# A two-block transformer step in split fp32: rounded-weight products with 512 moving columns in place of 256

## Chip, cores and metric

One NeuronCore of a Trainium2 chip. The metric is the device time of one execution in microseconds, here of the only core. `kernel` packs the weights on the host, builds one program and launches it once.

## What is computed

One batch row of 256 tokens and 1024 features goes through block 1 twice (its two layers) and then through block 2 twice. All inputs and the output are fp32. Cut to what matters:

```python
def layer_1(x):                       # twice
    s1, k1, g1, s2, k2, g2 = split(silu(c) @ w_ada + b_ada, 6)
    z = modulate(rmsnorm(x), s1, k1) @ w_in          # 1024 -> 2284 columns
    x = x + g1 * (concat(swa(z), mla(z), nsa(z), moba(z)) @ w_out)
    u = relu(modulate(rmsnorm(x), s2, k2) @ w_up) ** 2     # 1024 -> 4096
    return x + g2 * (u @ w_down)                           # 4096 -> 1024

def layer_2(x, mem):                  # twice
    z, xs, bc, dt, dq, dk, dv, dg, cq, cg, gl = split(x @ w_in_2)
    mk, mv = split(mem @ w_mem_kv)
    y = rmsnorm(ssd_scan(conv(xs), conv(bc), dt) * silu(z))     # 32 heads
    d = diff_attention(rope(dq), rope(dk), dv) * silu(dg)       # 8 heads
    q = cross_attention(cq, mk, mv) * silu(cg)                  # 4 heads
    g = sigmoid(gl + gate_b)                                    # three gates
    o = g[0] * (y @ w_br_ssd) + g[1] * (d @ w_br_diff) + g[2] * (q @ w_br_cross)
    return layernorm(alpha * x + o @ w_out_2)
```

## The kernel before, in words

Activations lie feature-major: a tile of 128 features by 256 tokens, eight of them for the 1024 features. A product with a weight keeps nearly fp32 accuracy by splitting both sides into a rounded part (type fp32r, one pass of the array) and the rest: `ah`, `al` for activations, `wh`, `wl` for weights, and summing `wh*ah + wh*al + wl*ah` in PSUM.

The weights come through one stream. `stream` (L269) lists weight groups of 1024x256 in the order of their use; each is two tiles `w` of 128x1024 (512 KB), loaded by SP's queue up to `AHEAD_W` = 8 tiles ahead (`_fetch`, L273). Up to four tiles ahead `_split` (L282) rounds them: ScalarE writes `wh` (L290), VectorE the rest `wl` (L292), both put ahead of other work by `high_priority`.

`gemm` (L320) is the product. It takes one of three `g` banks of PSUM (128x512 fp32) and walks two pieces, one per weight tile; each has four slices `k` of 128 input features and two halves `c` of the output, and each of these issues three matmuls of 256 columns through `mm` (L317): `wh` with `ah`, `wh` with `al`, `wl` with `ah`. With `tok=True` the sides are swapped: the activation slice is the weight of the array and 256 weight columns move, so that tokens lie on partitions. After the last piece `evac` reads the whole bank: a copy (`cq` L1244, `mk` L439, the block-1 projections L687 and L688), a `relu` and its square (L966 to L971), a `silu` (`silu2`, L1108), a gate's `tanh` (L1374), or a multiplication into the sum of branches (L1381 to L1388).

The pieces are put into a queue (`add`, L305) and the program calls `fill(n)` and `need(tag)` between the steps of attention, scan and norms, so that TensorE has products to run while the other engines work. From this emission order a scheduler sets the final order on each engine; engines run their lists in order.

The down product of the MLP (`down`, L975), the causal convolutions' products (`xs`, `bc`), `dt`, and `w_out1` have their own PSUM layout or readers and also use 256 columns. In block 2 the 32 scan heads (`scan_a`, `scan_b`) alternate with the pieces of `cg`, `gl`, `br2`, `xs`, `dq` and `dk`, the eight heads of the differential attention (`diff`, L1538) with those of `z` and `br0`; the products of `dg`, `gl`, `br1` and `out` follow one another.

Of the kernel before, what the change touches and what calls it, by code (L numbers as in the profile page):

```python
# [58 lines left out]
def _pack_in(w):  # L59

    L, K, M = w.shape
    r = w.reshape(L, K // P, P, M // 256, 256).transpose(0, 3, 2, 1, 4)
    return np.ascontiguousarray(r).reshape(L, M // 256, P, -1)

# [69 lines left out]
def _pack(inp):  # L134
# [39 lines left out]
    for key, n0, n in (("z", 0, 2048), ("xs", 2048, 2048), ("bc", 4096, 1024), ("dq", 5184, 1024), ("dk", 6208, 1024),  # L174
                       ("dv", 7232, 1024), ("dg", 8256, 1024), ("cq", 9280, 1024), ("cg", 10304, 1024), ("gl", 11328, 3072)):
        o["w2_" + key] = _pack_in(cut(n0, n))
    dt = np.concatenate([cut(5120, 64), np.zeros((DEPTH, D, 64), np.float32)], 2)
    o["w2_dt"] = dt.reshape(DEPTH, KC, P, P).transpose(0, 2, 1, 3).reshape(DEPTH, P, 1024)
    o["w2_mem"] = _pack_in(a["w_mem_kv_2"])
# [4 lines left out]
    o["w2_out"] = _pack_in(a["w_out_2"])  # L184
# [21 lines left out]
NW, NS = 8, 4  # L206
AHEAD_W, AHEAD_S = 8, 4
# [5 lines left out]
flat = lambda tl: tl.rearrange("p a b -> p (a b)")  # L213


class Emit:
# [52 lines left out]
    def stream(self, *keys):  # L269
        for key in keys:  # L270
            self.wq.extend([key, i, None, None] for i in range(1 if key[0] == "w2_dt" else 2))
# [48 lines left out]
    def gemm(self, tag, keys, act, evac, tok=False, half=None):  # L320
# [6 lines left out]
        def piece(n):  # L327
# [4 lines left out]
            ah, al = act(n // 2)  # L332
            for k in range(4):
                kk = (n % 2 if half is None else half) * 4 + k
                for c in range(2):
# [3 lines left out]
                    if tok:  # L339
                        sl = slice(k * 256, (k + 1) * 256)  # L340
                        ts = slice(c * P, (c + 1) * P)
                        self.mm(o, ah[:, kk, ts], wh[:, sl], st, False)
                        self.mm(o, al[:, kk, ts], wh[:, sl], False, False)
                        self.mm(o, ah[:, kk, ts], wl[:, sl], False, sp)
                    else:
                        sl = slice(k * 256 + c * P, k * 256 + (c + 1) * P)
                        self.mm(o, wh[:, sl], ah[:, kk, :], st, False)
                        self.mm(o, wh[:, sl], al[:, kk, :], False, False)
                        self.mm(o, wl[:, sl], ah[:, kk, :], False, sp)
# [3 lines left out]
        for n in range(last + 1):  # L353
            self.add(tag, lambda n=n: piece(n))
# [72 lines left out]
def load_mem(e):  # L427
    mf = v3(e.unit("mf"), KC)
    mh, ml = v3(e.unit("mh", F32R), KC), v3(e.unit("ml", F32R), KC)
    for k in range(0, KC, 4):  # L430
        e.nc.sync.dma_start(mf[:, k : k + 4, :], e.d["memT"][:, k : k + 4, :])
        e.split(mh[:, k : k + 4, :], ml[:, k : k + 4, :], mf[:, k : k + 4, :])
    return mh, ml


def mem_gemm(e, l, g, hl, mk, mv, tag="mem"):

    if g < 4:
        ev = lambda ps: e.nc.scalar.copy(mk[:, 2 * g : 2 * g + 2, :], v3(ps, 2))  # L439
    else:  # L440
        ev = lambda ps: e.nc.scalar.copy(mv[:, :, (g - 4) * 256 : (g - 3) * 256], v3(ps, 2))
    e.gemm(tag, [("w2_mem", l, g)], lambda i: hl, ev, tok=g >= 4)
# [3 lines left out]
def block1(e, ctx, mem0):  # L446
# [3 lines left out]
    mhl, mk0, mv0 = mem0  # L450
# [14 lines left out]
    MEM = 6  # L465
    a0 = ada(0, 0) + ada(0, 1)
    start = [[], a0[0:2], a0[2:4], a0[4:6], a0[6:8], []]
    for k in range(MEM):
        e.stream(("w2_mem", 0, k), *start[k])
# [13 lines left out]
    e.stream(*[("w2_mem", 0, k) for k in range(MEM, 8)])  # L483
# [63 lines left out]
    def norm_apply(src, bc, A, sh, ah, al):  # L547
        with tc.high_priority(offset=NORM_FIRST):
            for k in range(KC):
                tt = e.t(ap_, [P, S], "nt", bufs=2)  # L550
                nc.vector.scalar_tensor_tensor(tt, src[:, k, :], A[:, k : k + 1], bc[:, :S], ALU.mult, ALU.mult)
                nc.scalar.activation(ah[:, k, :], tt, AF.Identity, bias=sh[:, k : k + 1])  # L552
                nc.vector.scalar_tensor_tensor(al[:, k, :], tt, sh[:, k : k + 1], ah[:, k, :].bitcast(F32), ALU.add, ALU.subtract)  # L553


    for g in range(MEM):
        mem_gemm(e, 0, g, mhl, mk0, mv0, f"start{g}")
# [27 lines left out]
    class Attend:  # L585
# [70 lines left out]
        def out(self, put=None):  # L656
# [7 lines left out]
            if self.last:  # L664
                oh, ol, base = put
                for c in range(2):
                    e.split(oh[:, base + c, :], ol[:, base + c, :], o[c][:, :S])

    def mixers(l, ah, al, oh, ol, ev_x):
# [9 lines left out]
        def ev_c(ps):  # L679
# [6 lines left out]
        act = lambda i: (ah, al)  # L686
        dv = lambda dst: (lambda ps: nc.vector.tensor_copy(dst, ps if len(dst.shape) == 2 else v3(ps, 2)))  # L687
        sc = lambda dst: (lambda ps: nc.scalar.copy(dst, v3(ps, 2)))  # L688
        evs = {0: ("A", dv(zA)), 1: ("B", dv(zB)), 2: ("C", ev_c), 3: ("H", dv(vn)), 5: ("E", sc(qa)), 4: ("D", sc(qn)),
               6: ("F", sc(qm)), 7: ("G", dv(km)), 8: ("I", sc(vm))}  # L690
# [984 lines left out]
```

## Time and profile before

| | |
|---|---|
| time, median of 3 runs | 1840.06 us (1837.85 to 1841.8) |
| the profiled execution | 1838.83 us |
| its span, first to last instruction | 1837.0 us |
| TensorE busy | 98% of the span, 14800 records |
| VectorE / ScalarE / POOL busy | 73% / 55% / 20% |
| mean granted TensorE clock | 0.992 |
| read from HBM | 339 MB |

PE is TensorE's matmul, PEld its weight load (beside it), DVE is VectorE, ACT ScalarE, SP the engine that issues the loads. A name such as `g<-ah,wh` says which tiles an instruction writes and reads, without buffer numbers; a matmul's duration in the trace is a modelled latency, so the price of one in a stream is the distance between starts. Plain fp32 matmuls (attention scores, transposes) are recorded as two instructions.

### The profile page before, as it was taken

The numbers are of one execution on the slowest core, as the hardware profiler recorded it, in microseconds if no ns is written. First come the engines' busy times: TensorE is split into PE (matmuls) and PEld (weight loads), VectorE is DVE, ScalarE is ACT, GpSimd is POOL, SyncE is SP. The second block draws the span as 40 slices with busy tenths as digits, with TensorE's granted clock in tenths as the row PEclk, the third lists the DMA queues.
The fourth block names the chain that finished last, engine by engine and source line by source line (L and its number), as shares of the span: only waits on it lengthen the run. The fifth ranks groups of instructions, "written<-read, shape, count | busy, mean of one in ns | idle before, by whom it ended". The sixth has DMA issues, their size and how long they took to land.

```text
span 1837.0 us, 37186 instructions
## 1 busy us (share of the span) xinstructions
PE 1791.6 (98%) x14800; PEld 1696.7 (92%) x14800; DVE 1334.8 (73%) x2212; ACT 1017.1 (55%) x1882; POOL 358.9 (20%) x291
## 2 busy tenths in 40 slices
PE   7999999999998999999999999999999999999998
PEld 6878799987878999999999999999999999999998
DVE  4575775756778655798897897566687897997566
ACT  4354444444545444557777575454556687675552
POOL 0000271800007300002444202200001445202200
PEclk9999999999998999999999999999999999999999
DMA  9873886757447655554444644465553445554451
GB/s 335 317 246 129 301 272 197 258 197 294 130 138 282 230 182 183 168 171 140 143 162 154 191 161 148 166 205 175 193 175 130 148 160 162 181 166 168 153 183 60
DMA packets 98223, 346.88 MB, mean 189 GB/s; under 512 B 12288, under 2 KB 13440, under 8 KB 97792
## 3 DMA queue, kind: packets, MB, share of 16 engines
q1 hardware_dynamic: 98048, 344.50, 55.5%
q8 instruction: 116, 1.90, 0.4%
q14 instruction: 59, 0.48, 0.1%
HBM read 339.01 MB, written 1.05 MB: 185 GB/s over the span
## 4 chain that ended last, share of the span: by engine, by line
PE 90%; DVE 3%; ACT 2%; DMA 2%; issue 1%; POOL 0%; POOLq 0%; SPq 0%; DVEq 0%; ACTq 0%
PE g L318 68%; PE acc L318 10%; PE yps L318 2%; DVE wl L292 1%; PE sc L318 1%; PE ada L318 1%; PE ds L318 1%; PE o L318 1%; DMA w<-w_ada 1%; ACT wh L290 1%; PE do L318 1%; PE xs L318 1%; PE xo L318 1%; DMA w<-w_up 1%; PE tw L1153 1%
## 5 line engine op out<-in xcount | busy, mean ns | idle before, releaser
L292 DVE TENSOR_TENSOR wl<-w,wh 128x1024 fp32r<-128x1024 f32 x518 | 664.3, 1285 | 337.7 <-ACT wh L290 335.5
L290 ACT CAST wh<-w 128x1024 fp32r<-128x1024 f32 x518 | 540.6, 1047 | 510.9 <-PE g L318 328.3
L318 PE MATMUL g<-xh,wh 128*128 128x256 f32 x1664 | 477.1, 287 | 0.7 <-DVE cv L1234 0.4
L318 PE MATMUL g<-xl,wh 128*128 128x256 f32 x1664 | 472.3, 284 | 0.0
L318 PE MATMUL g<-xh,wl 128*128 128x256 f32 x1664 | 471.7, 284 | 0.0
L318 PEld LDWEIGHTS g<-xh,wh 128*128 128x128 f32 x1664 | 319.3, 192 | 13.0 <-issue 6.9
L318 PEld LDWEIGHTS g<-xl,wh 128*128 128x128 f32 x1664 | 319.4, 192 | 0.8 <-issue 0.7
L318 PEld LDWEIGHTS g<-xh,wl 128*128 128x128 f32 x1664 | 319.4, 192 | 0.1
L318 PE MATMUL g<-ah,wh 128*128 128x256 f32 x736 | 210.4, 288 | 4.2 <-ACT ah L552 4.2
L318 PE MATMUL g<-al,wh 128*128 128x256 f32 x736 | 210.6, 287 | 2.5 <-DVE al L553 2.5
L318 PE MATMUL g<-ah,wl 128*128 128x256 f32 x736 | 210.8, 287 | 0.7 <-DVE wl L292 0.7
L358 POOL TENSOR_TENSOR rsy<-rv,mhalf 128x2 f32<-128x2 f32 (+1 forms) x14 | 13.4, 958 | 938.8 <-DVE rv L375 831.1
L318 PE MATMUL acc<-pt,wh 128*128 128x256 f32 x1024 | 183.1, 280 | 0.0
L1452 POOL PARTITION_BROADCAST E<-rows x64 | 96.6, 1571 | 389.0 <-PE tw L1153 157.7
L1451 ACT ACTIVATE E<-E,ltok 128x128 f32<-128x128 f32 x384 | 124.5, 394 | 61.9 <-POOL E L1452 57.9
L318 PEld LDWEIGHTS acc<-pt,wh 128*128 128x128 f32 x1024 | 156.8, 188 | 0.4 <-issue 0.4
L318 PEld LDWEIGHTS g<-ah,wh 128*128 128x128 f32 x736 | 142.2, 194 | 8.0 <-ACT ah L552 4.4
L318 PEld LDWEIGHTS g<-al,wh 128*128 128x128 f32 x736 | 142.7, 194 | 4.5 <-DVE al L553 3.5
L318 PEld LDWEIGHTS g<-ah,wl 128*128 128x128 f32 x736 | 142.6, 194 | 1.3 <-DVE wl L292 1.1
L318 PE MATMUL acc<-pt,wl 128*128 128x256 f32 x512 | 142.3, 279 | 0.0
L531 POOL TENSOR_SCALAR sb<-w,ca 128x1024 f32<-128x1024 f32 x24 | 89.3, 3721 | 62.6 <-PE ada L318 32.8
L318 PEld LDWEIGHTS acc<-pt,wl 128*128 128x128 f32 x512 | 96.2, 188 | 0.0
(384 smaller groups left out, 3571.4 us busy)
## 6 DMA issues: line engine op xcount, KB each, us to landing
w<-w_ada SPq DMA_DIRECT2D x96, 512.0 KB
w<-w_up SPq DMA_DIRECT2D x64, 512.0 KB
w<-w_down SPq DMA_DIRECT2D x64, 512.0 KB
w<-w_br SPq DMA_DIRECT2D x64, 512.0 KB
w<-w_gl SPq DMA_DIRECT2D x48, 512.0 KB
w<-w_in SPq DMA_DIRECT2D x36, 512.0 KB
w<-w_mem SPq DMA_DIRECT2D x32, 512.0 KB
w<-w_out SPq DMA_DIRECT2D x32, 512.0 KB
```

The costliest lines, as they stand in the source:

```text
L290: nc.scalar.copy(wh, w)
L292: nc.vector.tensor_tensor(wl, w, wh.bitcast(F32), ALU.subtract)
L318: self.nc.tensor.matmul(o, l, r, start=start, stop=stop)
L358: self.nc.gpsimd.tensor_tensor(y, v, self.mhalf[:, 0:cols], ALU.pow)
L531: nc.gpsimd.tensor_scalar(dst, w, ca[:, 2 * n + i : 2 * n + i + 1], None, ALU.mult)
L1153: nc.tensor.transpose(tps[:, kt * S + t * P : kt * S + (t + 1) * P], src[:, t, kt * P : (kt + 1) * P], e.ident)
L1451: ex = lambda o, s, r: nc.scalar.activation(o, o, AF.Exp, bias=bias[:, s, r : r + 1])
L1452: nc.gpsimd.partition_broadcast(E, state["rows"][32 * (h % 4) : 32 * (h % 4) + 1, :])
```

## The change

`gemm` stays for the products that keep 256 columns. Two forms are new. `wide` lays both activation parts side by side (class `Pair`, 512 values behind one another by one step of the address pattern) and passes them as one moving side of 512 columns through `wh`, then `ah` alone through `wl`. Each output half `c` now has a bank of its own: columns 0 to 255 hold `wh*ah + wl*ah`, columns 256 to 511 `wh*al`. At the end ScalarE copies the second half to SBUF and VectorE adds the first; the consumers read that sum in SBUF, mostly in place. `tok_gemm` moves 512 weight columns past an activation slice, one bank for each half of the tokens. The weight tiles of `dv`, `mv` and the last `out` are packed 512 columns wide for it; six groups of memory weights stand in place of eight. Since the sums take a buffer of 4 KB per partition, the weight ring has seven tiles in place of eight.

```diff
-NW, NS = 8, 4
-AHEAD_W, AHEAD_S = 8, 4
+NW, NS = 7, 4
+AHEAD_W, AHEAD_S = 7, 4
+class Pair:
+    def __init__(self, e, name):
+        self.u = [e.unit(name, F32R).rearrange("p (j k s) -> p j k s", j=2, k=4) for _ in range(2)]
+    def part(self, j, k, n=1):
+        u = self.u[k // 4]
+        return u[:, j, k % 4, :] if n == 1 else u[:, j, k % 4 : k % 4 + n, :]
+    def both(self, k):
+        return self.u[k // 4][:, :, k % 4, :]
...
+    def wide(self, tag, keys, act, into, evac=None):
+        banks, dst = [], []
+        last = 2 * len(keys) - 1
+        def piece(n):
+            wh, wl = self.next_w(*keys[n // 2])
+            a = act(n // 2)
+            for c in range(2):
+                if n == 0:
+                    banks.append(self.gbank("g"))
+                ps = banks[c]
+                for k in range(4):
+                    kk = n % 2 * 4 + k
+                    sl = slice(k * 256 + c * P, k * 256 + (c + 1) * P)
+                    self.mm(ps, wh[:, sl], a.both(kk), n == 0 and k == 0, False)
+                    self.mm(ps[:, 0:S], wl[:, sl], a.h(kk), False, n == last and k == 3)
+                if n == last:
+                    if c == 0:
+                        dst.append(into())
+                    d = dst[0][:, c * S : (c + 1) * S]
+                    self.nc.scalar.copy(d, ps[:, S : 2 * S])
+                    self.nc.vector.tensor_tensor(d, ps[:, 0:S], d, ALU.add)
+            if n == last and evac:
+                evac(dst[0])
+        for n in range(last + 1):
+            self.add(tag, lambda n=n: piece(n))
+
+    def tok_mm(self, ps, t, a, k, w, j, st, sp):
+        wh, wl = (x[:, j * 512 : (j + 1) * 512] for x in w)
+        h, l = (x[:, t * P : (t + 1) * P] for x in (a.h(k), a.l(k)))
+        self.mm(ps, h, wh, st, False)
+        self.mm(ps, h, wl, False, False)
+        self.mm(ps, l, wh, False, sp)
+
+    def tok_gemm(self, tag, key, a, evac):
+        banks = []
+        def piece(n):
+            w = self.next_w(*key)
+            for t in range(2):
+                if n == 0:
+                    banks.append(self.gbank("g"))
+                for j in range(2):
+                    self.tok_mm(banks[t], t, a, 2 * n + j, w, j, n == 0 and j == 0, n == 3 and j == 1)
+                if n == 3:
+                    evac(banks[t], t)
...
-                e.gemm("mlp", [("w_up", l, g)], lambda i: (ah, al), ev_up(g))
+                e.wide("mlp", [("w_up", l, g)], lambda i: a2, lambda: e.t(ap_, [P, 512], "sum", bufs=2), ev_up(g))
...
-    def silu2(ps_, dst):
+    def silu2(s):
         th = e.t(tp_, [P, 512], "th", bufs=3)
-        nc.scalar.activation(th, ps_, AF.Tanh, scale=0.5)
-        nc.vector.scalar_tensor_tensor(dst, th, 1.0, ps_, ALU.add, ALU.mult)
+        nc.scalar.activation(th, s, AF.Tanh, scale=0.5)
+        nc.vector.scalar_tensor_tensor(s, th, 1.0, s, ALU.add, ALU.mult)
...
-            e.gemm("cq", G("cq", g), act, lambda ps, g=g: nc.scalar.copy(cq[:, 2 * g : 2 * g + 2, :], v3(ps, 2)))
+            e.wide("cq", G("cq", g), act, lambda g=g: flat(cq[:, 2 * g : 2 * g + 2, :]))
...
-                e.gemm(key, G(key, g), act, ev)
+                e.wide(key, G(key, g), act, cv_sum, ev)
...
-                e.gemm(tag, keys, parts, ev_br)
+                e.wide(tag, keys, parts, lambda: e.t(tp_, [P, 512], "sum", bufs=2), ev_br)
...
-            e.gemm("z", G("z", g), act, ev_z)
+            e.wide("z", G("z", g), act, cv_sum, ev_z)
```

In the same way the memory keys, seven of the nine block-1 projections, the gates (`gl`), `dq`, `dk`, `dg` and `out` of the first layer become `wide`; `mv`, `dv` and `out` of the last layer become `tok_gemm`.

What the scheduler makes of it on TensorE, in a product of `z` among the differential heads of the first block-2 layer (`x` is the activation, `g` its bank). Before:

```order
L318 MATMUL g_12493<-xh_8526,wh_12359 128x256
L318 MATMUL g_12493<-xl_8527,wh_12359 128x256
L318 MATMUL g_12493<-xh_8526,wl_12361 128x256
L318 MATMUL g_12493<-xh_8526,wh_12359 128x256
L318 MATMUL g_12493<-xl_8527,wh_12359 128x256
L318 MATMUL g_12493<-xh_8526,wl_12361 128x256
```

Of the change, from the last row of one bank over a transpose of attention weights (`tw`) to the first rows of the next bank:

```order
L349 MATMUL g_11479<-x_7899,wl_11389 128x256
L1251 MATMUL tw_11532<-pack_1_70,E_11313 128x128 x3
L349 MATMUL g_11488<-x_7898,wh_11354 128x512
L349 MATMUL g_11488<-x_7898,wl_11356 128x256
L349 MATMUL g_11488<-x_7898,wh_11354 128x512
L349 MATMUL g_11488<-x_7898,wl_11356 128x256
```

Three rows of 256 columns have become one of 512 and one of 256, and the product fills its first bank (16 rows, over both weight tiles) before it starts the second.

VectorE in the same place (`cv` is the product's sum or its `silu`, `wl` a weight split, `E`, `sm` and `sd` belong to the softmax, `ysl` to the split of the scan's output, `fold` to its norm). Before:

```order
L292 TENSOR_TENSOR wl_12581<-w_12401,wh_12579 128x1024
L1112 SCALAR_TENSOR_TENSOR cv_12554<-th_12555,g_12493 128x512
L1548 SCALAR_TENSOR_TENSOR E_12476<-E_12476,sd_12473,E_12484 128x256 x2
L292 TENSOR_TENSOR wl_12611<-w_12431,wh_12609 128x1024
L1483 SCALAR_TENSOR_TENSOR xsT_8577<-cv_12554,xsT_8577 128x512
```

Of the change:

```order
L323 TENSOR_TENSOR wl_11573<-w_11477,wh_11571 128x1024
L411 TENSOR_TENSOR cv_11585<-g_11553,cv_11585 128x256
L1238 TENSOR_REDUCE sm_11611<-ds_11605 128x2
L1210 SCALAR_TENSOR_TENSOR cv_11511<-th_11524,cv_11511 128x512
L1238 TENSOR_REDUCE sm_11619<-ds_11606 128x2
L323 TENSOR_TENSOR wl_11634<-w_11501,wh_11632 128x1024
L411 TENSOR_TENSOR cv_11585<-g_11562,cv_11585 128x256
```

Each product brings two additions (L411) between the weight splits, and its `silu` (L1210) reads the sum of a product whose banks are already free.

ScalarE there (`do` is attention output, `ysh` the rounded scan output, `th` a `tanh` or a square). Before:

```order
L290 CAST wh_12579<-w_12401 128x1024
L1111 ACTIVATE th_12555<-g_12493 128x512
L290 CAST wh_12609<-w_12431 128x1024
L1556 COPY dq_11574<-do_12569 128x256
L290 CAST wh_12675<-w_12498 128x1024
```

Of the change:

```order
L321 CAST wh_11571<-w_11477 128x1024
L410 COPY cv_11585<-g_11553 128x256
L1643 COPY dq_10662<-do_11538 128x256
L1209 ACTIVATE th_11524<-cv_11511 128x512
L321 CAST wh_11632<-w_11501 128x1024
L410 COPY cv_11585<-g_11562 128x256
```

The copies of the second halves (L410) stand between the roundings, one for each bank.

## Rows read from the trace of the kernel before

**Rows 1.** The page: span, busy time of each engine, the chain by engine and line.
```profile
span 1837.0 us, 37186 instructions
...
PE 1791.6 (98%) x14800; PEld 1696.7 (92%) x14800; DVE 1334.8 (73%) x2212; ACT 1017.1 (55%) x1882; POOL 358.9 (20%) x291
...
PE 90%; DVE 3%; ACT 2%; DMA 2%; issue 1%; POOL 0%; POOLq 0%; SPq 0%; DVEq 0%; ACTq 0%
PE g L318 68%; PE acc L318 10%; PE yps L318 2%; DVE wl L292 1%; PE sc L318 1%; PE ada L318 1%; PE ds L318 1%; PE o L318 1%; DMA w<-w_ada 1%; ACT wh L290 1%; PE do L318 1%; PE xs L318 1%; PE xo L318 1%; DMA w<-w_up 1%; PE tw L1153 1%
```

**Rows 2.** The chain of waits in order of time: start us, length us, what.
```profile
184.52 8.62 DMA w<-w_out
...
292.60 5.76 PE g L318 x48
298.36 5.66 PE acc L318 x48
...
547.28 8.16 DMA w<-w_up
...
1167.21 110.02 PE g L318 x917
```

**Rows 3.** Timeline of TensorE: start us, us from first start to last end, instruction.
```profile
1350.10 1.03 PE L318 MATMUL xs<-mk,cq 128*128 128x256 f32 x4
...
1733.99 0.28 PE L318 MATMUL xt<-identr,xh 128*128 128x128 f32 x1
1734.10 0.27 PE L318 MATMUL xt<-identr,xl 128*128 128x128 f32 x1
```

**Rows 4.** Stages: length, busy us and instructions of each engine, clock, DMA share, GB/s.
```profile
0.00:75.00 75.00, 63.66 (x547) 57.35 (x548) 35.84 (x56) 31.42 (x42) 1.81 (x5) 1.00 0.94 347
75.00:225.00 150.00, 143.12 (x1227) 116.84 (x1227) 99.68 (x289) 66.35 (x161) 10.62 (x6) 0.98 0.64 229
225.00:400.00 175.00, 174.78 (x1470) 172.94 (x1469) 114.85 (x97) 82.38 (x95) 87.53 (x28) 1.00 0.69 229
400.00:555.00 155.00, 142.99 (x1247) 120.48 (x1246) 105.10 (x297) 71.27 (x166) 3.76 (x4) 0.98 0.56 192
770.00:884.00 114.00, 113.57 (x896) 111.34 (x894) 99.93 (x185) 74.82 (x129) 9.39 (x12) 1.00 0.48 160
884.00:1103.00 219.00, 218.35 (x1768) 204.23 (x1768) 192.32 (x309) 160.66 (x362) 72.48 (x84) 1.00 0.50 162
1103.00:1170.00 67.00, 67.00 (x554) 64.85 (x553) 43.75 (x75) 36.38 (x84) 19.66 (x19) 1.00 0.46 150
1170.00:1321.00 151.00, 151.00 (x1262) 151.00 (x1261) 100.89 (x118) 75.33 (x94) 0.73 (x1) 1.00 0.57 189
1321.00:1438.00 117.00, 117.00 (x926) 115.10 (x926) 94.72 (x164) 72.46 (x124) 7.96 (x12) 1.00 0.47 156
1438.00:1658.00 220.00, 219.35 (x1779) 205.28 (x1778) 194.79 (x309) 160.48 (x363) 72.65 (x84) 1.00 0.51 163
1726.00:1837.00 111.00, 103.70 (x867) 103.50 (x865) 67.44 (x84) 44.69 (x56) 3.00 (x2) 0.98 0.38 128
```

**Rows 5.** Groups by form: busy us, mean ns of one, idle time before, releaser.
```profile
L318 PE MATMUL xs<-mk,cq 128*128 128x256 f32 x64 | 15.1, 379 | 0.0
...
L292 DVE TENSOR_TENSOR wl<-w,wh 128x1024 fp32r<-128x1024 f32 x518 | 664.3, 1285 | 337.7 <-ACT wh L290 335.5 <-DMA w<-w_ada 0.5 <-PE g L318 0.4
...
L1173 DVE TENSOR_TENSOR r<-g,r 128x256 f32<-128x256 f32 x8 | 3.2, 421 | 6.0 <-PE g L318 6.0
...
L290 ACT CAST wh<-w 128x1024 fp32r<-128x1024 f32 x518 | 540.6, 1047 | 510.9 <-PE g L318 328.3 <-PE acc L318 70.5 <-issue 50.6
...
L515 ACT COPY pt<-ada 128x256 f32<-128x256 f32 x12 | 4.5, 371 | 5.1 <-PE ada L318 5.1
...
L1244 ACT COPY cq<-g 128x512 f32<-128x512 f32 x8 | 4.6, 580 | 0.0
```

**Rows 6.** The fullest piece of the first long stage, columns as in rows 4.
```profile
1042.00:1103.00 61.00, 61.00 (x502) 58.79 (x502) 57.55 (x116) 44.32 (x107) 0.00 (x0) 1.00 0.49 161
```

More of the change, by code (lines that the diff above doesn't have):

```diff
@@ L270, in stream @@
         for key in keys:
-            self.wq.extend([key, i, None, None] for i in range(1 if key[0] == "w2_dt" else 2))
+            self.wq.extend([key, i, None, None] for i in range(self.d[key[0]].shape[-1] // 1024))
     def _fetch(self, ent):
@@ L464, in block1 @@
     mlp_keys = lambda l: {1 + 6 * i + n: [("w_ada", *p, n)] for i, p in enumerate(ad_mlp(l)) for n in range(4)}
-    MEM = 6
+    MEM = 5
     a0 = ada(0, 0) + ada(0, 1)
-    start = [[], a0[0:2], a0[2:4], a0[4:6], a0[6:8], []]
+    start = [[], a0[0:2], a0[2:4], a0[4:6], a0[6:8]]
     for k in range(MEM):
-        e.stream(("w2_mem", 0, k), *start[k])
+        e.stream(MEM_KEYS(0)[k], *start[k])
     for l in range(DEPTH):
@@ L482, in block1 @@
         e.stream(("w_down", l, 15), *([("w_in1", l + 1, zorder[0])] if l + 1 < DEPTH else []), *ad_next(l))
-    e.stream(*[("w2_mem", 0, k) for k in range(MEM, 8)])
+    e.stream(*MEM_KEYS(0)[MEM:])
     th = e.t(cp, [P, KC], "cth")
@@ L695, in z_gemm @@
             g = zorder[i]
-            tag, ev = evs[g]
-            e.gemm(tag, [("w_in1", l, g)], act, ev, tok=g in (3, 8))
+            key = [("w_in1", l, g)]
+            if g in evs:
+                e.gemm(evs[g][0], key, act, evs[g][1], tok=True)
+            elif intos[g][1] is None:
+                e.wide(intos[g][0], key, act, lambda: e.t(ap_, [P, 512], "sum", bufs=2), ev_c)
+            else:
+                e.wide(intos[g][0], key, act, lambda: intos[g][1])
         def out_gemm(tag, j):
             for g in (2 * (j % 2), 2 * (j % 2) + 1):
-                e.gemm(tag, [("w_out1", l, j)], lambda i: (oh, ol), ev_x(g), half=j // 2)
+                e.gemm(tag, [("w_out1", l, j)], lambda i: ot, ev_x(g), half=j // 2)
         def out_quarter(j, i):
@@ L856, in mixers @@
         swa.turn()
-        swa.out((oh, ol, 0))
+        swa.out((ot, 0))
         e.fill(1)
@@ L868, in mixers @@
         mla.turn()
-        mla.out((oh, ol, 2))
+        mla.out((ot, 2))
         e.need("F")
@@ L926, in mixers @@
         win.turn()
-        win.out((oh, ol, 4))
+        win.out((ot, 4))
         e.need("I")
@@ L930, in mixers @@
         moba.turn()
-        moba.out((oh, ol, 6))
+        moba.out((ot, 6))
         e.need("o3")
@@ L1029, in block1 @@
             nc.vector.scalar_tensor_tensor(x[:, k, :], acc[k // 2][:, (k % 2) * S : (k % 2 + 1) * S], mod[:, 40 + k : 41 + k], x[:, k, :], ALU.mult, ALU.add)
-    for k in range(MEM, 8):
+    for k in range(MEM, 6):
         mem_gemm(e, 0, k, box[0], mk0, mv0)
@@ L1119, in block2 @@
             e.stream(a, b)
-        for a, b in zip(W("xs"), W("dv")):
-            e.stream(a, b)
+        for g, a in enumerate(W("xs")[0:4]):
+            e.stream(a, *W("dv")[g // 2 : g // 2 + g % 2])
         for g, a in enumerate(W("cg")):
@@ L1131, in block2 @@
             e.stream(("w2_gl", l, 4 + g), ("w2_br1", l, g))
-        e.stream(*W("out"))
+        e.stream(*(W("out") if l + 1 < DEPTH else [("w2_last", 0, g) for g in range(2)]))
         if l + 1 < DEPTH:
-            e.stream(*[("w2_mem", l + 1, g) for g in range(8)])
+            e.stream(*MEM_KEYS(l + 1))
     def soft(scs, scale):
```

224 lines of the change are left out of this document (114 added, 110 removed).

## The prediction

> **What bounds the kernel now.** I read the page first, then the chain of waits, the stages, and last the single matmuls. The page has TensorE busy for 98% of the span, VectorE for 73%, ScalarE for 55%, and the chain that ended last lies on TensorE for 90%, 68% of the span in the products into the `g` banks alone [rows 1]. So the price of a `g` matmul is the price of the kernel, unless another engine is nearly as full in some stage. The chain shows that price: 48 matmuls of 256 columns in 5.76 us, 917 in 110.02 us, that is 0.120 us each; in the down products (`acc`) 48 take 5.66 us, 0.118 us each [rows 2]. At the granted clock of 1.00 (the 2.4 GHz level) 256 columns stream in 256/2.4 = 0.107 us, so 0.013 us of each matmul is something else. Two rows tell what. The `xt` matmuls of 128 columns, which stream in 0.053 us, still start 0.11 us apart: a fresh 128x128 weight block costs about 0.11 us however few columns pass it. And the `xs` matmuls in plain fp32, which occupy the array twice as long for 256 columns, as long as 512 rounded ones would, start (1.03 - 0.38)/3 = 0.217 us apart with the same weight load beside them: only 0.004 us above the 0.213 us of streaming [rows 3, 5]. A weight load is therefore hidden under a long stream, and nearly as long as a stream of 256.
>
> VectorE is the rival resource, and by stage, not by average. In the scan and attention stages of block 2 (884 to 1103 and 1438 to 1658 us) it is busy 192.3 of 219 us and 194.8 of 220 us, while it has over 30% free in the first MLP and from 1103 to 1321 us [rows 4].
>
> **TensorE's part of the change.** A wide product does with two matmuls (512 and 256 columns) what three of 256 did. Before, 3 x 0.120 = 0.360 us. After, 0.217 for the 512 (nearest row: `xs`) and 0.119 for the 256, whose successor's weights load under it as now: 0.336 us. Bounds for the unseen 512: 0.213 us, the streaming alone, and 0.240 us, two of the present matmuls, which would make the pair 0.359 us and the gain nil; I take 0.217 because `xs` has the same array time and the same weights. The diff makes 170 weight groups of 1024x256 wide (8 for the memory keys, 14 in `w_in1`, 32 in `w_up`, 56 in each layer of block 2, 4 in `out`), each of 16 such triples: 2,720 x 0.024 = 65.3 us, 0.384 us a group. The token-major products (`mv`, `dv`, last `out`; 20 old groups) go from 960 x 0.120 to 480 x 0.217 us: 11.0 us, 0.55 us an old group. Together 76.3 us of TensorE time; what reaches the end depends on the stage:
> - 0 to 75 us: the DMA share is 0.94 [rows 4], so the 2.7 us that the first memory products lose are waited for all the same. Nothing.
> - 75 to 225 and 400 to 555: 14 groups, 5.4 us. TensorE idles 7 and 12 us there [rows 4], behind attention steps; I count half, 2.7 us.
> - The MLPs: 32 groups and the late `mv`, 13.4 us, all on the path (TensorE 174.8 of 175 us, VectorE 114.9 [rows 4]).
> - 770 to 884 and 1321 to 1438: `cq` and `dv`, 3.7 us each, 7.5 us.
> - 1103 to 1170 and 1658 to 1726: 12 groups each, 9.2 us. 1170 to 1321: 20 groups and `mv`, 9.9 us. From 1726: 12 groups and the last product, 6.8 us.
>
> That is 49.5 us. The remaining 21.5 us belong to the 28 groups in each of the two VectorE stages.
>
> **VectorE's and ScalarE's part.** Every wide product ends with a ScalarE copy and a VectorE addition for each of two halves; the consumers stay, in place. Nearest rows: 0.421 us for an addition of 256 from PSUM to SBUF and 0.371 us for such a copy [rows 5]. So 0.84 us of VectorE and 0.74 us of ScalarE a product, 162 products (the 8 of `br0` use two groups each). The old whole-bank copies that go (38 of 0.58 us on ScalarE [rows 5], six on VectorE) give a little back. VectorE rises by about 131 us to 1466, ScalarE by 98 to 1115. Outside the two stages this is hidden: in the MLPs each product adds 0.84 us per 11.4 us, and behind 1103 VectorE goes from 43.8 to 50.5 of 62 us. Inside them it is not: 28 x 0.84 = 23.6 us make 192.3 + 23.6 = 215.9 and 194.8 + 23.6 = 218.4 us of VectorE, 434.3 in all, where TensorE would need only 208 + 209 = 417. VectorE becomes the bound there. From 1042 to 1103 it is already busy for 57.5 of 61 us without holding TensorE [rows 6]; if it can be filled to 0.975, the stages take 434.3/0.975 = 445.4 us against 439 now: **6.4 us lost** where 21.5 were to be had. ScalarE, at 161 + 21 us in each, stays below.
>
> **Waits that the change moves.** A product now holds two of three `g` banks, not one. Behind the late bank queue the next product's matmuls in TensorE's order, behind the copy its addition, and behind that the consumer. The chain is 0.37 + 0.42 us, plus at worst one weight rounding on each engine (1.05 and 1.29 us [rows 5]): 3.1 us. In the order, 16 matmuls or so (2.7 us) of the other bank lie between the end of a bank and its next use. I take 0.03 us for each of the 106 products outside the two stages, 3 us; bounds 0 and 0.2 us each, 21 us. Weight tiles go from eight ahead to seven. The chain has four transfers between stages on it, the longest 8.62 and 8.16 us [rows 2]; one tile less loaded ahead is 512 KB, 1.5 us at the 347 GB/s of the first stage, so 0 to 6 us; I take 4. The tail keeps its length: two additions and two statistics of 512 in place of four each.
>
> **Sum.** The profiled execution took 1838.8 us (span 1837.0; the median shown is 1.2 us higher). 1838.8 - 49.5 + 6.4 + 3 + 4 = 1802.7, or **1803 us**.
>
> One page of the Trainium skill would have it otherwise. For 512 columns the row nearest in array time says 0.217 us [rows 3]. "TensorE: Matmul & The Clock Gate", section "Back-to-back issue gap", gives 131 ns per matmul of 512 columns in a stream of loads and matmuls, and N/2.4 + 2.5 ns, 216 ns here, for the isolated gap. By the second my sum stands; by the first a triple would take 0.250 us, and the sum would be near the last rival below.
>
> **Rivals.**
> - *VectorE's surplus moves on.* The 12 us that VectorE has free behind 1103 and 1658 take the additions that are late, and the two stages run at TensorE's pace: 1838.8 - 49.5 - 21.5 + 7 = 1775 us. For it: the weight splits run ahead of their use. Against: the diff and scan steps need their own results in place.
> - *Slower: VectorE can't be filled.* The scan's exponentials pass POOL, ScalarE and VectorE in turn, and every consumer now waits for one more handover. If VectorE reaches only 0.88, the two stages take 493.5 us (+54.5) and the `cq` to `dv` stages lose their 7.5 us: 1838.8 - 42 + 54.5 + 7 = 1858 us. It decides from a filling of about 0.90 down (481 us). For it: it is at 0.88 of the first long stage now [rows 4]; against: it isn't pushed there.
> - *512 columns cost two of 256*, or the two-part moving operand costs what it saves: no TensorE gain, 1838.8 + 6.4 + 7 = 1852 us. For it: no 512-column rounded matmul is in the trace. Against: `xs`.
> - *A wide matmul costs hardly more than one of 256*, 0.120 us: a group then saves 16 x 0.120 = 1.92 us, and outside the long stages and the start, with half of the 14 of block 1, 103 groups save 198 us, the token-major ones 8. VectorE holds back some 20 of it (behind 1103 it needs 50.5/0.975 = 52 us where TensorE would need 44, up to 1321 121 for 111): 1838.8 - 198 - 8 + 20 + 6.4 + 7 = 1666 us. Against: the two rows of 256 columns are at 0.118 and 0.120 us, hardly above their 0.107 us of streaming. The 131 ns of the Trainium skill's page would be this case.
>
> That the products aren't wide can be left aside: the order shows the 512-column rows.
>
> **Chances.** My forecast with its spread of small waits 0.56 (1785 to 1822); surplus moved on 0.15; between forecast and no change, with VectorE filled to 0.91 or 0.93, 0.05; no change within 0.2%, which is about what a measurement of this kernel can tell from none, 0.04; VectorE not filled 0.11; no column gain 0.07; wide matmuls at the price of narrow ones 0.02. So faster 0.56 + 0.15 + 0.05 + 0.02 = 0.78, same 0.04, slower 0.18. The range 1768 to 1850 leaves out the last rival, the longer half of the unfilled case and half of the column case.
>
> **What would show it.** Right: wide matmuls starting 0.217 us before the 256 behind them, 48-matmul pieces of MLP replaced by pieces of 5.4 us, VectorE at 0.95 or more of the two long stages with TensorE waiting for `wl`, `cv` or `sum` there, and these stages about as long as now. Wrong: 0.24 us for 512 columns; waits of TensorE on `g` banks all over the stages behind 1103; VectorE below 0.92 in the long stages while these are longer than 230 us; or VectorE's new additions far from 0.42 us.

## The result and the profile after

The changed kernel takes 1884.9 us (median of 4 runs, 1883.3 to 1886.1), the kernel before 1840.9 (4 runs): a ratio of 1.0241, 95% interval 1.0223 to 1.0259. It is **slower by 2.4%**; 1803 us was forecast, and the range ended at 1850. The profiled execution took 1886.1 us, with a span of 1884.3.

The page of the changed kernel, first lines and chain:

```profile
span 1884.3 us, 31369 instructions
...
PE 1793.7 (95%) x11600; PEld 1534.3 (81%) x11600; DVE 1447.8 (77%) x2522; ACT 1104.1 (59%) x2170; POOL 362.7 (19%) x291
...
PE 79%; DVE 8%; ACT 4%; DMA 4%; issue 2%; POOL 1%; SPq 1%; POOLq 0%; DVEq 0%; ACTq 0%
```

Against [rows 1]: 3,200 matmuls fewer (2,720 of the triples and 480 token-major ones), and TensorE is as long busy as it was (1793.7 for 1791.6 us). It now idles 1884.3 - 1793.7 = 90.6 us, where it idled 45.4, and VectorE and ScalarE have entered the chain. The mean granted clock fell from 0.992 to 0.977: at the two levels that rows show, about 2 x 0.023 x 1884 = 87 us of half clock for about 29 before (89 and 31 us by the clock's own stretches in the traces).

**The price of a wide matmul.** The timeline of TensorE in the changed kernel, at the granted clock of 1.00; the second column is how long a row lasts as the trace models it, so the starts are what counts:

```profile
1230.24 0.28 PE L349 MATMUL g<-x,wl 128*128 128x256 f32 x1
1230.36 0.40 PE L349 MATMUL g<-x,wh 128*128 128x512 f32 x1
1230.59 0.28 PE L349 MATMUL g<-x,wl 128*128 128x256 f32 x1
1230.71 0.40 PE L349 MATMUL g<-x,wh 128*128 128x512 f32 x1
```

A pair takes 0.35 us, 0.233 for the 512 columns and 0.117 for the 256 (medians over the 2,576 and 2,476 of them at full clock that follow each other without idle time). The triple before took 0.360. So a triple gains 0.009 us, not 0.024: 2,720 x 0.009 = 24.5 us, and the token-major matmuls (0.227 us each) 480 x (0.240 - 0.227) = 6 us. That is 31 us of TensorE for the 76 that the forecast had.

**The sums' own price** was as forecast: two rows of the groups by form (mean ns of one behind the busy time; then the idle time before them):

```profile
L411 DVE TENSOR_TENSOR sum<-g,sum 128x256 f32<-128x256 f32 x116 | 48.2, 417 | 5.8 <-ACT sum L410 5.7
L410 ACT COPY sum<-g 128x256 f32<-128x256 f32 x116 | 42.5, 368 | 34.0 <-PE g L349 34.0
```

**Where TensorE waits.** Behind 774 us (block 2) it idles 39.2 us, 11.1 of them behind its last matmul; in block 2 of the kernel before it idled 9.1, 7.3 of them at the end. The longest waits there:

```profile
PE g L349 <- DVE gt L411: 9.5, 4, 3.2
PE g L349 <- DVE sum L411: 5.4, 4, 2.1
PE g L349 <- ACT mv L533: 3.9, 1, 3.9
PE yps L349 <- DVE E L1549: 3.6, 3, 2.0
```

L411 is the addition of a wide product. One such wait, from end to end, in three timelines of the second scan stage: ScalarE, VectorE, TensorE.

```profile
1518.20 0.35 ACT L410 COPY gt<-g 128x256 f32<-128x256 f32 x1
1518.45 0.56 ACT L1322 ACTIVATE cv<-g,pack 128x256 f32<-128x256 f32 x1
1518.91 1.98 ACT L321 CAST wh<-w 128x1024 fp32r<-128x1024 f32 x2
1520.80 0.37 ACT L410 COPY gt<-g 128x256 f32<-128x256 f32 x1
```

```profile
1519.90 1.39 DVE L1449 SCALAR_TENSOR_TENSOR cv<-cv,cq 128x512 f32<-128x512 f32 x1
1521.22 0.41 DVE L411 TENSOR_TENSOR gt<-g,gt 128x256 f32<-128x256 f32 x1
1521.55 1.06 DVE L1549 TENSOR_TENSOR E<-E,gm 128x512 f32<-128x512 f32 x1
1522.54 0.47 DVE L1325 SCALAR_TENSOR_TENSOR cv<-g,pack,cv 128x254 f32<-128x254 f32 x1
1522.93 0.47 DVE L1561 SCALAR_TENSOR_TENSOR xsT<-xsT,pack,yps 128x256 f32<-128x256 f32 x1
1523.32 0.83 DVE L1549 TENSOR_TENSOR E<-E,gm 128x512 f32<-128x512 f32 x1
1524.07 3.27 DVE L323 TENSOR_TENSOR wl<-w,wh 128x1024 fp32r<-128x1024 f32 x2
1527.26 0.41 DVE L411 TENSOR_TENSOR gt<-g,gt 128x256 f32<-128x256 f32 x1
```

```profile
1521.68 0.50 PE L349 MATMUL g<-yc,wh 128*128 128x512 f32 x1 [1.30 <-DVE gt L411]
...
1527.72 0.80 PE L349 MATMUL g<-yc,wh 128*128 128x512 f32 x1 [2.38 <-DVE gt L411]
1528.32 0.41 PE L349 MATMUL g<-yc,wl 128*128 128x256 f32 x1
1528.53 0.63 PE L349 MATMUL g<-yc,wh 128*128 128x512 f32 x1
1528.96 0.41 PE L349 MATMUL g<-yc,wl 128*128 128x256 f32 x1
```

The first copy starts at 1518.20; between the two copies stand a convolution step and two weight roundings. VectorE does the first addition at 1521.22, 2.7 us after that copy's end; it had been busy up to then. The second half's copy ends at 1521.17, its addition runs at 1527.26, behind six other instructions. TensorE stands for 1.30 us, and then for 2.38. Behind the second pause a pair takes 0.43 + 0.21 us, the price of the 1.2 GHz level. Over all 324 halves, the time from the copy's start to the addition's end is 2.1 us in the mean (median 1.7), where the two instructions take 0.79; in 84 of them it is over 2.7 us. Over the whole run TensorE waits 18.2 us for additions, 13.1 of them for one that stood behind a weight split (`wl`) when its copy was done.

**Where the time went by stage**, in us, each from a mark in the trace: the last matmul of `acc` (down products), the first of `dt`, ScalarE's first write of `yd`:

| stretch | before | change | no additions | four banks | mixed |
|---|---|---|---|---|---|
| start to the last `acc` of layer 0 | 403.8 | 415.1 | 408.8 | 425.7 | 399.4 |
| to `dt` of block 2 | 356.7 | 359.3 | 352.8 | 364.3 | 356.8 |
| to the first `yd` (cq to attention) | 427.5 | 446.5 | 427.0 | 431.1 | 428.8 |
| to `dt` of layer 1 | 130.3 | 135.1 | 127.2 | 127.3 | 126.3 |
| to the first `yd` of layer 1 | 428.6 | 434.9 | 428.7 | 430.5 | 428.9 |
| to the end | 90.0 | 93.3 | 89.4 | 94.5 | 88.0 |

Block 1 lost 14 us, block 2 33 us. The last three columns are experiments 1, 8 and 12.

### The profile page after: what moved, and what is told of

The parts are those of the page before. It is cut to its first block, busy times and chain, and to the rows that moved or that the text cites. A ratio compares the mean times of both kernels' runs of the same rounds, so it can differ in the third digit from the quotient of the medians.

```text
span 1884.3 us, 31369 instructions
## 1 busy us (share of the span) xinstructions
PE 1793.7 (95%) x11600; PEld 1534.3 (81%) x11600; DVE 1447.8 (77%) x2522; ACT 1104.1 (59%) x2170; POOL 362.7 (19%) x291
## 4 chain that ended last, share of the span: by engine, by line
PE 79%; DVE 8%; ACT 4%; DMA 4%; issue 2%; POOL 1%; SPq 1%; POOLq 0%; DVEq 0%; ACTq 0%
PE g L349 58%; PE acc L349 9%; DVE wl L323 4%; ACT wh L321 2%; PE ada L349 1%; ACT E L1540 1%; PE yps L349 1%; DMA gt<-cv 1%; PE o L349 1%; PE ds L349 1%; PE sc L349 1%; PE do L349 1%; POOL E L1541 1%; DMA w<-w_ada 1%; ACT sb L718 1%
## 5 line engine op out<-in xcount | busy, mean ns | idle before, releaser
L349 PE MATMUL g<-x,wh 128*128 128x512 f32 (+1 forms) x2048 | 600.5, 358 | 4.1 <-DVE sum L411 2.9
L349 PE MATMUL g<-x,wl 128*128 128x256 f32 x1664 | 465.8, 282 | 0.0
L349 PEld LDWEIGHTS g<-x,wh 128*128 128x128 f32 x2048 | 359.9, 190 | 69.4 <-DVE cv L411 5.1
L349 PEld LDWEIGHTS g<-x,wl 128*128 128x128 f32 x1664 | 315.9, 190 | 3.0 <-issue 0.8
L349 PE MATMUL g<-a,wh 128*128 128x512 f32 x736 | 271.9, 410 | 16.6 <-DVE a L644 14.5
L349 PE MATMUL g<-a,wl 128*128 128x256 f32 x736 | 208.8, 286 | 1.7 <-DVE wl L323 1.7
L349 PEld LDWEIGHTS g<-a,wh 128*128 128x128 f32 x736 | 141.6, 193 | 54.5 <-DVE a L644 14.5
L349 PEld LDWEIGHTS g<-a,wl 128*128 128x128 f32 x736 | 142.7, 194 | 3.6 <-DVE wl L323 2.8
L349 PE MATMUL g<-ys,wh 128*128 128x512 f32 x256 | 91.3, 398 | 0.8 <-DVE ys L511 0.8
L1325 DVE SCALAR_TENSOR_TENSOR cv<-g,pack,cv 128x254 f32<-128x254 f32 (+1 forms) x192 | 88.0, 474 | 3.1 <-ACT cv L1322 1.9
```

Of the source, the lines that this page charges most:

```text
L349: self.nc.tensor.matmul(o, l, r, start=start, stop=stop)
L1325: nc.vector.scalar_tensor_tensor(a_[:, a:b], p_[:, a + j - 2 : b + j - 2], conv_w[:, i0 + j : i0 + j + 1], a_[:, a:b], ALU.mult, ALU.add)
```

## The experiments

**1. Without the additions.**

```diff
-                    self.nc.scalar.copy(d, ps[:, S : 2 * S])
-                    self.nc.vector.tensor_tensor(d, ps[:, 0:S], d, ALU.add)
+                    self.nc.scalar.copy(d, ps[:, 0:S])
```

> Left out: the VectorE addition of every wide product; ScalarE copies the first half of the bank alone, so the part of the rounded weights times the activations' remainder is missing from the sums. Products, banks and copies stay. Theory A (late sums): in the changed kernel TensorE idles 90.6 us of the span against 45.4 before, and its clock is halved for 89 us against 31, because matmuls wait for a bank that a copy and a queued addition have not yet read. Without the additions the idle time falls to 45 to 60 us, the halved time to 30 to 50 us, and the run takes 1800 to 1835 us. Theory B (the loss is not in the evacuation: one weight tile fewer, later transfers, dearer matmuls): idle time stays above 75 us and the run above 1860 us.

Measured: 1835.0 us, 0.9962 of before (0.9948 to 0.9976). Its page:

```profile
span 1833.7 us, 30981 instructions
...
PE 1770.0 (97%) x11600; PEld 1520.5 (83%) x11600; DVE 1344.2 (73%) x2198; ACT 1103.2 (60%) x2168; POOL 348.9 (19%) x291
```

Idle 63.7 us, a little above what theory A had; clock 0.989. Theory B falls: the loss hangs on the evacuation. But with 31 us cheaper products only 5 us are won against before: TensorE still idles 18 us more than it did. Of its waits, the ones for the split `a` in block 1 (6.7 us before), for the weight roundings (9.6) and for the copies of `cv` (none) have grown most:

```profile
PE g L349 <- ACT wh L321: 14.3, 3, 11.3
PE g L349 <- DVE a L643: 12.2, 3, 5.7
...
PE g L349 <- ACT cv L410: 4.4, 3, 2.1
```

The last are waits for the one copy that is left, so an evacuation of one instruction into SBUF is not free either.

**2. Both parts in one run of 512.**

```diff
-"p (j k s) -> p j k s", j=2, k=4)
+"p (k j s) -> p k j s", k=4, j=2)
```

> Both activation parts of a chunk lie side by side in SBUF, so the moving operand of a wide matmul is one run of 512 columns and not two of 256 that lie 4 KB apart; nothing else is changed. Wide matmuls now start 231 ns (median) before the 256 columns behind them, the token-major ones, whose 512 columns are one run, 226. Theory C (the two-part operand costs): 226 ns in the wide ones too, 2,720 x 0.005 = 14 us less, 1871 us. Theory D (512 columns cost this much however they lie): 231 ns stays, 1880 to 1890 us.

Measured: 1882.6 us, ratio 1.0241 (1.0214 to 1.0267); the wide matmul still starts 233 ns before its successor. The layout costs nothing. A 512 followed by another of 512 (token-major) is at 227; why one followed by a 256 is at 233 stays open.

**3 and 5. The token-major products alone, with eight and with seven weight tiles.** All other products go back to `gemm` and their old evacuations; `NW` and `AHEAD_W` are 8 in the first, 7 in the second.

> Every feature-major product is made as before (three matmuls of 256, one bank, no added copy or addition), with eight weight tiles ahead; what is left of the change are the token-major products with 512 weight columns moving (mv, dv, the last output) and the paired storage of the parts. 960 x 0.120 = 115.2 us become 480 x 0.227 = 109.0 us: 6 us less TensorE, of which the 1.6 us of mv in the first stage are hidden. Theory A: 1834 to 1839 us, halved clock about 31 us. Rival: the paired storage or the larger token-major pieces cost by themselves: above 1845 us.

> The kernel of e3_token_major_only (1837.4 us) with seven weight tiles ahead in place of eight; its products are the same. Theory A (late sums made the loss): the seventh tile is worth little, 1837 to 1842 us. Theory W (one weight tile fewer made much of it, since the long stages of e4_narrow_long_stages came back in the second layer alone): 1848 us or more.

Measured: 1837.4 us (ratio 0.9989, 0.9978 to 1.0001) and 1840.8 (1.0002, 0.9987 to 1.0017). Theory A both times. The weight tile is worth 3.4 us by the medians, though the two intervals overlap; in the traces the stretch up to the last `acc` of layer 0 is 9 us longer with seven (408.7 for 399.6), and block 2 is 3 us shorter.

**4. The long stages narrow.** `cg`, `gl` and `br` of branches 2 and 0, `dq`, `dk` and `z` by `gemm` again, the rest wide, seven tiles.

> The products of the scan and attention stages of block 2 (cg, gl of branches 2 and 0, br2, br0, dq, dk, z) are made as before; the rest stays wide, seven weight tiles. From the first scan product to the first yd of both layers the kernel before took 300 and 306 us, the changed one 326 and 323. Theory A (VectorE, nearly full there, is late with the sums): both stretches come back to 298 to 310 us, the run takes 1835 to 1850 us. Theory B (weight tiles or the matmuls' price): they stay above 315 us each and the run above 1865 us.

Measured: 1861.6 us (ratio 1.0116), between the two. By the first `yps` to the first `yd` the stretches are 315 and 317 us, which looked like theory B. But the stage in front had become shorter, 111 us for 121 in layer 1, because the marker had moved: from `cq` to `yd` they are 434.6 and 427.8, for 427.5 and 428.6 before. The second long stage had come back, the first for 12 of its 19 us; a stretch that begins at a moving mark misled the expectation. What is left of the loss is 15 us in block 1 and 8 us in block 2.

**6 and 7. Eight tiles with everything wide, and wide only where VectorE has room.**

```diff
-                r = e.t(ap_, [P, 512], "pt1", bufs=2)
-                nc.scalar.activation(r, ps, AF.Relu)
...
-                last["act"] = nc.scalar.activation(uh, r, AF.Square)
-                nc.vector.tensor_tensor(r, r, ps, ALU.mult)
+                nc.vector.scalar_tensor_tensor(r, r, 0.0, r, ALU.max, ALU.mult)
+                last["act"] = nc.scalar.copy(uh, r)
```

> The changed kernel with eight weight tiles: their room comes from the sum tiles (the branch sums go into a buffer of the scan, the MLP's sums into the tile that held the relu, whose square is then taken by VectorE with one instruction as before and rounded by ScalarE, one ScalarE instruction fewer per product), and from one product of each first-block layer that is made as before. All other products are wide. Theory A: 1868 to 1886 us. Theory W: 1860 us or less.

> Wide only where VectorE has over 30% free: memory keys, the MLPs, cq, and the last third of each block-2 layer (dg, gl and br of branch 1, out), 72 groups; eight weight tiles, the room made as in e6_wide_8_tiles. If sums cost nothing there, the gain is what the matmuls give: 72 x 16 x 0.0105 = 12 us below e3_token_major_only, 1823 to 1829 us. If their handover makes TensorE pause there too (it idles 6 us and is at half clock for 10 us between 1221 and 1356 us of the changed kernel): 1832 to 1842 us.

Measured: 1885.0 us (1.0250, 1.0219 to 1.0281) and 1846.9 (1.0038, 1.0018 to 1.0058). The eighth tile saves nothing in the wide kernel: theory W falls. In the second the MLPs gain what was hoped (169.6 us for 173.9 in layer 0), and pauses of 1 to 4 us at the second up product, at `cq`, at `out` and at the late memory values take it back. So free time on VectorE alone does not decide. The step behind the up product is a shorter one in both kernels, as the diff shows; what that gives by itself was not measured.

**8. Four banks for the products in block 2.**

```diff
+            e.ps, e.pg, e.nb, e.ng = pool("ps2"), pool("pg2"), 4, 4
```

> The changed kernel with four banks for the products and four for the rest in block 2 (three and five before); block 1 is as in the change. If a late sum holds TensorE up only because its bank is not free, the pauses in the two long stages and behind them go (17 us idle and 17 us at half clock in the scans, 6 and 10 us from 1221 to 1356 us): 1855 to 1872 us. If VectorE itself is the limit, or the consumers are: 1878 us or more.

Measured: 1873.8 us (1.0186, 1.0156 to 1.0215), a little above the first case; block 2 alone went from 1109.8 to 1083.3 us. Block 1, whose products and banks are the same, took 790 for 774 in another order; that part is not explained. So 26 of block 2's 33 us go with a fourth bank, though the sums come no earlier there: 2.6 us over all halves from the copy's start to the addition's end, for 2.1. TensorE's waits for additions fall from 18.2 to 9.9 us all the same. So these 26 us were in the main waits for a bank that the sums held.

**9. Two matmuls of 256 in place of each 512.**

```diff
-                    self.mm(ps, wh[:, sl], a.both(kk), n == 0 and k == 0, False)
+                    self.mm(ps[:, 0:S], wh[:, sl], a.h(kk), n == 0 and k == 0, False)
+                    self.mm(ps[:, S : 2 * S], wh[:, sl], a.l(kk), False, False)
```

> The changed kernel with each matmul of 512 columns made as two of 256 into the two halves of the same bank; banks, copies, additions, weight tiles and order rules stay. So only the price of the matmul differs: 3 x 0.120 us in place of 0.233 + 0.117. If the columns give what the starts say, 9 to 10 ns for each of 2,720 triples, and most of it counts, 1900 to 1911 us. If the pauses of the changed kernel swallow TensorE's gain (the sums set the pace): 1883 to 1892 us.

Measured: 1878.1 us (1.0209, 1.0192 to 1.0226), below both cases. Its page:

```profile
span 1881.2 us, 36809 instructions
...
PE 1809.4 (96%) x14320; PEld 1683.2 (89%) x14320; DVE 1450.6 (77%) x2522; ACT 1104.4 (59%) x2170; POOL 349.2 (19%) x291
```

The wide products have all their old matmuls back, 24.5 us of work for TensorE, and the kernel is no slower: idle time falls to 71.8 us and the clock rises to 0.984. The 512 columns bring nothing here. Against experiment 5, which has the same matmuls in these products, the same weight tiles and the old evacuation, it is 37 us slower: the 2% is the way in which the products are evacuated.

**10. Block 1's first products narrow** (`w_in1` by `gemm`).

> The changed kernel with the seven feature-major products of w_in1 in each layer of block 1 made as before; seven weight tiles, everything else wide. Up to the first down product the changed kernel takes 245 us, the token-major one with seven tiles 235, with eight 226. If late sums of these products hold the attention steps and their followers up: 233 to 238 us up to there, and 1868 to 1878 us in all. If the weights (a transfer-bound start, one tile fewer) or the norms make the difference: above 241 us and 1881 us or more.

Measured: 1876.2 us (1.0190). Up to the first down product 238.2 us for 245.0: as the first theory had it, though at its edge.

**13 to 15. Sums first, one bank at a time, sums first with four banks.** In 13 the copy and the addition stand under `high_priority(offset=150)`; in 14 a piece takes both weight tiles and one half; 15 is 13 with the banks of 8.

> The changed kernel with the copy and the addition of each wide product put ahead of the weight roundings in the scheduler's priorities (an offset of 150 where the roundings have 100). Theory Q (the sums are late because they queue behind roundings of 1.0 and 1.3 us): TensorE's idle time falls from 90.6 us to about 65 and its halved time from 89 us to about 50, 1850 to 1868 us. Theory V (VectorE's and ScalarE's total work, or the roundings that are now late in their turn): 1878 us or more.

> The changed kernel with the halves of a one-group product made one behind the other: the first half takes both weight tiles and all eight chunks in one bank, then the second half in another, so the first bank's copy and addition run during the second half and a product holds one bank at a time (br0, of two groups, stays). Theory B (two of three banks held at once make the pauses): 1855 to 1870 us. Theory Q or V: the sums are late whatever bank they wait in, and each first half now needs its second weight tile 2.8 us earlier: 1880 us or more.

> e13_sums_first with the four g banks in block 2 of e8_four_g_banks (1873.8 us). If queue and banks are two separate causes, block 2 (from the first dt product to the end 1110 us in the changed kernel, 1083 with four banks, 1076 before) comes to 1060 to 1072 us, and the run to 1825 to 1855 us. If they are one cause seen twice, block 2 stays at 1078 us or more.

Measured: 1884.8 (1.0243), 1877.5 (1.0201) and 1865.4 us (1.0132). In block 2 they take 1107, 1106 and 1084 us, for 1110 in the changed kernel and 1083 with four banks. 13 comes out as theory V had it, but it is no test of theory Q: the higher priority did not bring the sums forward. From the copy's start to the addition's end they take 2.1 us in the mean, as in the changed kernel, and behind 105 of the 324 copies (106 there) a weight split still starts before the addition; with four banks it is 127 in both 15 and 8. Why the scheduler left them there is not known. So the queue behind the roundings, which the timelines above show, stays a possible cause of the late sums, and no run here has taken it away. 14 did change the order (the second copy of a product starts 3.7 us behind the first in the median, 2.3 before); its sums take 2.1 us all the same, and it wins 7 us, 4 of them in block 2. That falls between its two theories: to give the first bank back earlier is not enough by itself.

**17. VectorE alone.** As in 1 a part of the sum is left out, but now VectorE does the work.

```diff
-                    self.nc.scalar.copy(d, ps[:, S : 2 * S])
-                    self.nc.vector.tensor_tensor(d, ps[:, 0:S], d, ALU.add)
+                    self.nc.vector.tensor_copy(d, ps[:, 0:S])
```

> Left out, as in e1_no_add, is the part of the rounded weights times the activations' remainder; but here VectorE copies the first half of each bank and ScalarE does nothing, so that VectorE keeps an instruction per half (about 0.4 us, as the addition took) and the handover from ScalarE to VectorE is gone. Theory V (VectorE's time for the sums is what TensorE waits for): 1868 us or more. Theory H (the chain of two engines): 1830 to 1848 us, as without the additions (1835).

Measured: 1841.3 us (1.0007, 0.9995 to 1.0018). Its page, and its window of the first scan and attention stage (length, then busy time and instructions of PE, PEld, DVE, ACT, POOL, and the granted clock), with the same stage of the kernel before and of the changed one behind it:

```profile
span 1842.7 us, 31087 instructions
...
PE 1779.3 (97%) x11600; PEld 1526.4 (83%) x11600; DVE 1451.0 (79%) x2522; ACT 1007.5 (55%) x1846; POOL 361.6 (20%) x291
```

```profile
885.00:1198.00 313.00, 310.46 (x1879) 259.35 (x1879) 277.05 (x473) 206.28 (x449) 93.63 (x103) 1.00 0.49 163
```

```profile
884.00:1188.00 304.00, 303.35 (x2469) 287.08 (x2469) 246.00 (x393) 204.54 (x452) 92.13 (x103) 1.00 0.50 161
```

```profile
893.00:1221.00 328.00, 318.77 (x1888) 265.05 (x1887) 277.94 (x475) 229.00 (x526) 90.01 (x103) 0.98 0.49 158
```

VectorE does as much as in the changed kernel, 277 us of this stage and 1451 in all, and 43 us are gone. So its load is not the bound. (The 31 us of cheaper matmuls don't show here either: TensorE idles 63.4 us, as in 1.) Experiments 1 and 17 each take away one engine's share, and in both the loss is nearly gone; what both lack is the second step, the handover from ScalarE to VectorE while the bank is held. ScalarE's load fell too in 17, and VectorE's in 1. A kernel in which both engines do their instruction side by side, with the full load and no handover, was not tried; so whether it is the order of the two steps or their number that holds the bank so long stays open.

**11, 12 and 16. A version that beats both.** The kernel of 3 with the MLPs' up products wide from the third on, with the shorter step of 6 behind them (11); with `dg` and both products of branch 1 wide as well (12); and with their sums first (16).

```diff
-                e.gemm("mlp", [("w_up", l, g)], lambda i: a2, ev_up(g))
+                if g >= 2:
+                    e.wide("mlp", [("w_up", l, g)], lambda i: a2, lambda: e.t(ap_, [P, 512], "pt1", bufs=2), ev_up(g))
+                else:
+                    e.gemm("mlp", [("w_up", l, g)], lambda i: a2, ev_up(g))
```

> The kernel of e3_token_major_only (eight tiles, token-major products of 512, 1837.4 us) with the MLPs' up products from the third one on made wide (28 groups); the sum lies in the tile of the relu as in e6_wide_8_tiles. e7_wide_where_room took 169.6 us from the first to the last down product of layer 0 where e3_token_major_only took 173.9, and 182.8 for 186.2 behind layer 1; the first two products stay as before because TensorE paused for 3.4 and 2.8 us there. 28 x 16 x 0.009 = 4.0 us at least, 7 to 8 us if the stages shorten as there: 1829 to 1834 us. Rival: the sums cost a pause elsewhere, 1836 us or more.

> e11_wide_mlp with dg and both products of branch 1 wide as well in both layers of block 2 (24 groups), where VectorE is at 80% or below. cq, the memory keys and out stay as before, because TensorE paused for 1 to 4 us at each of them in e7_wide_where_room. 24 x 16 x 0.009 = 3.5 us below e11_wide_mlp: 1825 to 1831 us. Rival: late sums at the ends of these pieces make pauses of 1 to 2 us with halved clock behind: no gain, or slower than e11_wide_mlp by up to 5 us.

> e12_wide_mlp_and_diff_out (1829.3 us) with its sums ahead of the roundings. TensorE idles there little (12.7 us in block 2), so little is to be had: 1825 to 1830 us. If the roundings become late in turn: above 1832 us.

Measured: 1833.3 us (0.9952, 0.9937 to 0.9968), 1829.3 (0.9942, 0.9926 to 0.9959) and 1831.1 (0.9943, 0.9925 to 0.9961): 0.5 to 0.6% faster than before, the first two as forecast. 11 is 4 us below 3, with intervals that don't overlap; 12 is not clearly below 11. In 16 VectorE and ScalarE run the same instructions in the same order as in 12, so it is a repeat of 12, with the same ratio, and says nothing of the priority. The page of 12:

```profile
span 1828.2 us, 34726 instructions
...
PE 1778.4 (97%) x13488; PEld 1627.3 (89%) x13488; DVE 1375.6 (75%) x2308; ACT 1031.6 (56%) x1958; POOL 364.8 (20%) x291
```

## Why the prediction was wrong, step by step

- **The 512-column matmul, 0.217 us by the `xs` row: mis-sized.** It takes 0.233, 0.227 behind another of its kind. The nearest row in array time was not near enough: it was a plain fp32 matmul of 256 columns, and nothing in the trace showed that the rounded form adds only 4 ns to its streaming. Of 0.024 us a triple 0.009 were there; 31 us for 76. The bounds, 0.213 to 0.240, held. Of the page's two figures in the Trainium skill ("TensorE: Matmul & The Clock Gate", section "Back-to-back issue gap"), 216 ns is nearer than 131, and the trace is above both.
- **"I take 0.03 us for each of the 106 products", 3 us with bounds 0 and 21: the step that failed.** TensorE idles 45 us more and is about 58 us longer at half clock, which costs up to half of that again. The text had the parts: a worst chain of 3.1 us, and 2.7 us of other matmuls between a bank's end and its next use. It then priced the worst case as rare. It is not: the sum takes 2.1 us from the copy's start in the mean, before any wait for that copy, and over 2.7 us in a quarter of the cases. Leaving out either step takes away 27 of the 45 us, and 48 (experiment 1) or 28 us (17) of the half clock. Three banks with two in each product leave too little room in block 2, as experiment 8 shows; what makes the sums late, the roundings in the queues or the handover itself, is not separated.
- **No price was put on a pause's clock.** The trace of the change has 16 stretches at half clock for 5 before, all but the one at the very end during or right behind a pause of TensorE of 0.8 us or more. [Rows 4] of before had such stages (clock below 1.00 where TensorE idled), so the term could have been read there.
- **"VectorE becomes the bound" in the long stages: the wrong mechanism.** They did lose: 19 and 6 us by the stretches up to `yd`, which hold the `cq` stages too, where 6.4 in both were forecast. That the size is near is luck: VectorE was busy for only 277.9 of 328 us, 0.85 where the text had 0.975, and experiment 17 runs the same load 15 us faster. The rival "VectorE can't be filled" was nearest in time (1858 us) and named the handover; it gave it a chance of 0.11 and looked for it in these two stages alone.
- **Right:** VectorE's and ScalarE's prices per sum (417 and 368 ns for 0.421 and 0.371; VectorE rose by 113 us for 131, ScalarE by 87 for 98), and the seventh tile (3.4 us for 4). Not the tail, which was to keep its length: from the last matmul to the end it is 11.1 us for 7.3.
- **Block 1:** of its attention stages I counted half the gain; there the wide products lost instead, about 7 us by experiment 10. In the MLPs, where [rows 4] had VectorE far from full, all of the gain was to come. By the stretches of the two layers (first to last down product, and first down product to `dt`) it was 4.3 and 0.3 us, in all the 32 x 16 x 0.009 = 4.6 us of the real price. That they add up is partly luck: each layer's share would be 2.3, and with the same matmuls and no additions (experiment 1) the first takes 174.2 us, for 174.4 before and 170.1 with the change.

How the miss of 82 us divides: of the 49.5 us that the sum took off for TensorE about 20 were there at the real price (49.5 x 31/76, an estimate), which leaves about 53 us for the pauses and the clock behind them. Experiment 9 puts it shortest: with the old matmuls and the new evacuation the kernel is as slow as with the new ones.

## What to carry to other kernels

Price an evacuation by how long it holds its bank, through every queue that it passes, and not by the busy time that it adds: with one instruction on one engine the kernel was about where it had been (1835 and 1841 us), the 31 us of cheaper matmuls spent; with two on two engines in turn it was 2.4% slower. Where TensorE is full, a change that saves it a few per cent must not make it pause, for the clock takes the pause a second time. Make such a change first where the products are long and alike (the MLP), and go on from there stage by stage. And when an experiment moves something in an order, read from its trace that it moved: experiment 13 was to bring the sums forward and did not, so its time says nothing about them.

## What the runs showed of the hardware

At the granted clock of 1.00 a rounded matmul of 256 columns starts 0.120 us after its like (0.107 of streaming), one of 512 columns 0.227 to 0.233 (0.213). At half clock the same rows are at 0.213 and 0.427 us, the streaming alone: what a matmul costs beside its columns at full speed, 13 to 20 ns, is gone there. A moving operand of two runs of 256 columns, 4 KB apart, costs no more than one run of 512 (experiment 2).
